# Activation tiles of a layer kernel moved by 8 to 256 bytes, and one product's columns walked backwards

## The chip, the core and the metric

The kernel runs on one core of one Trainium2 chip. The metric is the device time of one execution in microseconds (us); lower is better. Before the change the median of two runs is 2103.69 us (2103.62 to 2103.77).

## What is computed

One layer on a sequence of 256 rows of width 2048, in float32: a gated feed-forward block, a mixer with an attention branch and a gating branch, and a second feed-forward block. Cut to what matters here:

```python
x = x + 0.5 * swiglu(rms_norm(x, norm_ffn1), ffn1_w_gate, ffn1_w_up, ffn1_w_down)
h = rms_norm(x, norm_mix)
proj = h @ w_in                      # 2048 -> 10320 columns: q, k, v, index, u, v, gates
...                                  # attention with 64 picked keys; spatial gating
merged = sigmoid(ga) * (y_a @ w_up_attn) + sigmoid(gb) * (y_b @ w_up_sgu)
x = x + merged @ w_out
x = x + 0.5 * swiglu(rms_norm(x, norm_ffn2), ffn2_w_gate, ffn2_w_up, ffn2_w_down)
# swiglu(h, g, u, d) = (silu(h @ g) * (h @ u)) @ d ; inner width 5632
```

## The kernel before

Nearly all of the time goes into matrix products of 256 rows of activations with weights that are streamed from HBM once. One function, `gemm`, does each of them. For every block of 128 rows of the inner dimension (index `k`) the weights of 1024 output columns (1104 in one product) arrive by DMA in a tile `w`. ScalarE rounds them to the type float32r into `wh` (line 227), VectorE subtracts and writes what is left into `wl` (line 228). The activations are kept in the same manner as two float32r tiles, a high part and a low part, transposed: `xTh` and `xTl` hold the normed input of a stage (16 blocks of 128 by 256), `hTh` and `hTl` the inner activations of a feed-forward block (44 blocks).

A product of float32 accuracy is then three matrix products, lines 279 to 281: high activations by `wh`, low activations by `wh`, high activations by `wl`. In each, the activations are the stationary operand (128 by 128, loaded by a weight load of its own, LDWEIGHTS on PEld) and 512 columns of the weights are the moving operand (368 columns in the first product of the mixer). The result is added up in a PSUM bank `acc`. For one `k` there are two halves of the rows (`t`) and two blocks of columns (`j`), so 12 matrix products of 512 columns.

The stages stand one after the other:

- first block, gate and up: `acc<-wh,xTh` and its two companions, 11 chunks x 16 `k` x 12 = 2112 matrix products;
- first block, down: `acc<-wh,hTh`, 2 halves x 44 `k` x 12 = 1056;
- mixer, index columns: 288 of 368 columns, stationary operand from `xTh` and `xTl`;
- mixer, q, k, v, u, v and gates: 1728 of 512 columns from `xTh` and `xTl`, with the attention's small products strewn among them;
- mixer, three products with other activation tiles (`yah`, `ybh`, `mh`): 768;
- second block, gate and up: 2112; second block, down: 1056.

The class `Normed` makes `xTh` and `xTl` (lines 335 and 336 write them, ScalarE the high part and VectorE the low one). It is instantiated three times, for the first block, the mixer and the second block (`gi` is 0, 1 and 2), each time in the same memory. `ffn` makes `hTh` and `hTl`, written by lines 227 and 228 after a transposing DMA.

Where the tiles lie, in bytes from the start of a partition of SBUF, as the built program has it: `xTh` at 35840, `xTl` at 52224, the buffers of `wh` and `wl` from 93184 on in steps of 4096, `hTh` at 138240, `hTl` at 183296. All are multiples of 512. A stationary block is 512 bytes of a partition and begins at a multiple of 512; a moving block is 2048 bytes and begins 0 or 2048 bytes into a buffer (1472 bytes: 368 columns, at 0 or 1472). The distance between a moving and a stationary block, taken modulo 512 bytes, is 0 in every product of 512 columns.

Of the kernel before, what the change touches and what calls it, by code (L numbers as in the profile page):

```python
# [14 lines left out]
F32R = mybir.dt.float32r  # L15
# [6 lines left out]
P = 128  # L22
S = 256
NT = S // P
D = 2048
KD = D // P
FF = 5632
KF = FF // P
# [38 lines left out]
def block_kernel(ctx: ExitStack, tc: tile.TileContext, x, positions, norm_ffn1, ffn1_w_gate, ffn1_w_up,  # L67
# [5 lines left out]
    act = ctx.enter_context(tc.tile_pool(name="act", bufs=1))  # L73
# [9 lines left out]
    def uid(s):  # L83
        cnt[0] += 1
        return f"{s}_{cnt[0]}"

    def ttile(shape=None):
        return tmp.tile(shape or [P, 512], F32, tag="t", name=uid("t"))
# [4 lines left out]
    def bank(shape=None):  # L93
        return psA.tile(shape or [P, 512], F32, tag="acc", name=uid("acc"))
# [7 lines left out]
    def later(*stages):  # L102
        pending.extend(stages)

    def tick(n=1):
        for _ in range(min(n, len(pending))):
            pending.popleft()()
# [118 lines left out]
    def split_to(hi, lo, src):  # L226
        nc.scalar.copy(hi, src)  # L227
        nc.vector.tensor_sub(lo, src, hi.bitcast(F32))  # L228

    def gemm(xh, xl, nk, load, widths, first=0, rate=1, lead=None):  # L230

        ncol = sum(widths)
        kmax = 2048 // ncol
        banks = [[None] * len(widths) for _ in range(NT)]
        k0 = 0
        while k0 < nk:
            kg = min(1 if k0 < first else kmax, nk - k0)
            w = wraw.tile([P, 2048], F32, tag="w", name=uid("w"))
            wv = w[:, :kg * ncol].rearrange("p (k c) -> p k c", k=kg)
            load(k0, kg, wv)  # L240
            for kk in range(kg):
                k = k0 + kk

                offs = []
                o = 0
                for wd in widths:
                    offs.append(o)
                    o += wd
                parts = []
                cur = []  # L250
                for j, wd in enumerate(widths):
                    if cur and offs[j] + wd - offs[cur[0]] > 1024:
                        parts.append(cur)
                        cur = []
                    cur.append(j)
                parts.append(cur)
                hl = {}
                for part in parts:
                    a = offs[part[0]]
                    n = sum(widths[j] for j in part)  # L260
                    whi = wsp.tile([P, 1024], F32R, tag="wh", name=uid("wh"))
                    wlo = wsp.tile([P, 1024], F32R, tag="wl", name=uid("wl"))
                    with ExitStack() as order:
                        if lead is not None and k == 0:
                            for ins in lead:
                                order.enter_context(tc.issue_after(getattr(ins, "ins", ins)))
                        split_to(whi[:, :n], wlo[:, :n], wv[:, kk, a:a + n])
                    for j in part:
                        b = offs[j] - a
                        hl[j] = (whi[:, b:b + widths[j]], wlo[:, b:b + widths[j]])  # L270
                for t in range(NT):
                    sh = xh(k, t)
                    sl = xl(k, t)
                    for j, wd in enumerate(widths):
                        if k == 0:
                            banks[t][j] = bank()
                        o_ = banks[t][j][:, :wd]
                        whj, wlj = hl[j]
                        nc.tensor.matmul(o_, sh, whj, start=(k == 0), stop=False)  # L279
                        nc.tensor.matmul(o_, sl, whj, start=False, stop=False)  # L280
                        nc.tensor.matmul(o_, sh, wlj, start=False, stop=(k == nk - 1))  # L281
                tick(rate)
            k0 += kg
        return banks

    def loader(wap, c0, ncol):
        def load(k0, kg, dst):
            nc.sync.dma_start(dst, wap[k0 * P:(k0 + kg) * P, c0:c0 + ncol].rearrange("(k p) c -> p k c", p=P))
        return load
# [23 lines left out]
    class Normed:  # L313


        def __init__(self, gi):
            self.gi = gi
            self.h = act.tile([P, KD, S], F32R, tag="xTh", name=uid("xTh"))
            self.l = act.tile([P, KD, S], F32R, tag="xTl", name=uid("xTl"))
            self.ss = small.tile([P, NT, 4], F32, tag="ss", name=uid("ss"))  # L320
            self.rstd = small.tile([P, NT], F32, tag="rstd", name=uid("rstd"))

# [47 lines left out]
        def xh(self, k, t):  # L370
            return self.h[:, k, t * P:(t + 1) * P]

        def xl(self, k, t):
            return self.l[:, k, t * P:(t + 1) * P]

    def ffn(nrm, wg, wu, wd, after_chunk, first=0, lead=None):
        with tc.tile_pool(name=uid("ffn"), bufs=1) as pool:
            hTh = pool.tile([P, KF, S], F32R, name=uid("hTh"))
            hTl = pool.tile([P, KF, S], F32R, name=uid("hTl"))
            for fc in range(FF // 512):  # L380
                def load(k0, kg, dst, fc=fc):
                    for i, wap in enumerate((wg, wu)):
                        nc.sync.dma_start(dst[:, :, i * 512:(i + 1) * 512],
                                          wap[k0 * P:(k0 + kg) * P, fc * 512:(fc + 1) * 512].rearrange(
                                              "(k p) c -> p k c", p=P))
                b = gemm(nrm.xh, nrm.xl, KD, load, [512, 512], first=first if fc == 0 else 0, lead=lead if fc == 0 else None)
                for t in range(NT):
                    sg = ttile()
                    nc.scalar.activation(sg, b[t][0], AF.Silu, scale=nrm.rstd[:, t:t + 1])  # L389
                    hh = ttile()  # L390
                    nc.vector.scalar_tensor_tensor(hh, b[t][1], nrm.rstd[:, t:t + 1], sg,  # L391
                                                   op0=ALU.mult, op1=ALU.mult)
                    later(partial(turn_split, hTh[:, fc * 4:fc * 4 + 4, t * P:(t + 1) * P],
                                  hTl[:, fc * 4:fc * 4 + 4, t * P:(t + 1) * P], hh))
            for half in range(2):
                b = gemm(lambda k, t: hTh[:, k, t * P:(t + 1) * P], lambda k, t: hTl[:, k, t * P:(t + 1) * P],
                         KF, loader(wd, half * 1024, 1024), [512, 512])
                for t in range(NT):
                    for j in range(2):
                        xs = xres[:, t, (half * 2 + j) * 512:(half * 2 + j + 1) * 512]  # L400
                        nc.vector.scalar_tensor_tensor(xs, b[t][j], 0.5, xs, op0=ALU.mult, op1=ALU.add)  # L401
                        if t == NT - 1 or after_chunk is to_out:
                            after_chunk(half * 2 + j, t)
# [4 lines left out]
    lead = n1.pair(0)  # L408
# [19 lines left out]
    def to_out(c, t):  # L428
        nc.sync.dma_start(out[0, t * P:(t + 1) * P, c * 512:(c + 1) * 512], xres[:, t, c * 512:(c + 1) * 512])

    ffn(n1, ffn1_w_gate[0], ffn1_w_up[0], ffn1_w_down[0], to_mix, first=2, lead=lead)
    nm = nm[0]
    win = w_in[0]


    def mixer(pool, after_chunk):
# [30 lines left out]

        raw = mt("A", [P, NT, 1152], name="qik")
        b = gemm(nm.xh, nm.xl, KD, loader(win, C_QI, QIK), [368, 368, 368])
        flush()  # L470
        for t in range(NT):
# [297 lines left out]


    ffn(n2, ffn2_w_gate[0], ffn2_w_up[0], ffn2_w_down[0], to_out)


# [20 lines left out]
```

## Time and profile before

| | |
|---|---|
| median of two runs | 2103.69 us |
| the profiled execution | 2102.13 us |
| its span, first to last instruction | 2100.4 us |
| TensorE matmul (PE) busy | 2084.0 us, 99% |
| weight loads (PEld) busy | 1732.7 us, 82% |
| VectorE (DVE) busy | 1165.4 us, 55% |
| ScalarE (ACT) busy | 1038.5 us, 49% |
| HBM read | 398.26 MB |

How to read it: matrix products are pipelined, and the profile shows each from its start to the end of its last result, so that the time of one overlaps the next. A busy share of 99% says that there is always one under way, not how fast they follow each other. That is read from the distance between the starts of two neighbours in the timeline, or from the length of a stage over the number of its products.

### The profile page before, as it was taken

The page shows a single profiled execution, that of the slowest core. Times are in us where ns is not written, and L with a number is a line of the kernel's source. Part 1 is how long each engine was busy: PE and PEld are TensorE (multiplying, and loading weights), DVE is VectorE, ACT ScalarE, POOL GpSimd, SP SyncE. Part 2 cuts the span into 40 slices and gives each one's busy share as a digit, 9 for nine tenths or more (in the row PEclk, how much of TensorE's full clock was granted, in tenths as well). Part 3 has the DMA queues.
Part 4 walks back from the last instruction along what each step waited for, and adds up shares of the span by engine and source line. Part 5 has one row for each costly group of instructions (what it writes and reads, how often), then busy time and mean ns, then how long its engine had stood idle before and what let it go on. Part 6 is the DMA issues. An engine that isn't in the chain of part 4 may idle for free.

```text
span 2100.4 us, 24401 instructions
## 1 busy us (share of the span) xinstructions
PE 2084.0 (99%) x9318; PEld 1732.7 (82%) x9318; DVE 1165.4 (55%) x1362; ACT 1038.5 (49%) x1208; POOL 31.7 (2%) x60
## 2 busy tenths in 40 slices
PE   8999999999999999999999999999999999999998
PEld 6888888888888898888888888888888888888887
DVE  6555555555455457887544467555555555554443
ACT  5554444544345366567444445665444454443333
POOL 1000000000000000210000000000000000000000
PEclk9999999999999999999999999999999999999999
DMA  7666666666566477586665567676666666665654
GB/s 244 192 202 220 199 209 202 201 217 202 190 203 206 168 226 201 182 240 176 209 204 186 197 199 222 204 230 202 214 204 199 209 196 217 209 199 192 220 188 133
DMA packets 251526, 426.09 MB, mean 203 GB/s; under 512 B 106664, under 2 KB 108768, under 8 KB 251408
## 3 DMA queue, kind: packets, MB, share of 16 engines
q1 hardware_dynamic: 250880, 423.29, 63.7%
q0 software_dynamic: 528, 1.23, 0.3%
q8 instruction: 73, 1.20, 0.2%
q14 instruction: 45, 0.37, 0.1%
HBM read 398.26 MB, written 2.10 MB: 191 GB/s over the span
## 4 chain that ended last, share of the span: by engine, by line
PE 53%; ACT 0%; DMA 0%; DVE 0%; issue 0%; DVEq 0%
PE acc L279 17%; PE acc L281 17%; PE acc L280 17%; PE tr L687 0%; DMA tu<-pl 0%; DVE xres L401 0%; ACT L664 0%; PE tr L646 0%; ACT wh L227 0%; DVE pTs L299 0%; ACT vs L664 0%; DVEq L790 0%; ACT lgs L626 0%; ACT yah L227 0%; ACT pl L295 0%
## 5 line engine op out<-in xcount | busy, mean ns | idle before, releaser
L228 DVE TENSOR_TENSOR wl<-w,wh 128x1024 fp32r<-128x1024 f32 (+2 forms) x768 | 918.8, 1202 | 762.5 <-ACT wh L227 755.7
L227 ACT CAST wh<-w 128x1024 fp32r<-128x1024 f32 (+2 forms) x768 | 792.7, 1036 | 972.9 <-PE acc L280 957.3
L279 PE MATMUL acc<-wh,xTh 128*128 128x512 f32 (+1 forms) x2080 | 807.1, 388 | 3.4 <-ACT wh L227 3.4
L280 PE MATMUL acc<-wh,xTl 128*128 128x512 f32 (+1 forms) x2080 | 804.9, 387 | 0.0
L281 PE MATMUL acc<-wl,xTh 128*128 128x512 f32 (+1 forms) x2080 | 690.2, 387 | 0.0
L279 PEld LDWEIGHTS acc<-wh,xTh 128*128 128x128 f32 x2080 | 391.1, 188 | 81.8 <-ACT wh L227 4.7
L280 PEld LDWEIGHTS acc<-wh,xTl 128*128 128x128 f32 x2080 | 391.2, 188 | 76.6
L281 PEld LDWEIGHTS acc<-wl,xTh 128*128 128x128 f32 x2080 | 388.8, 188 | 77.3 <-DVE wl L228 0.6
L279 PE MATMUL acc<-wh,hTh 128*128 128x512 f32 x704 | 273.9, 389 | 0.0
L280 PE MATMUL acc<-wh,hTl 128*128 128x512 f32 x704 | 273.9, 389 | 0.0
L281 PE MATMUL acc<-wl,hTh 128*128 128x512 f32 x704 | 240.8, 389 | 0.0
L280 PEld LDWEIGHTS acc<-wh,hTl 128*128 128x128 f32 x704 | 132.2, 188 | 27.5
L281 PEld LDWEIGHTS acc<-wl,hTh 128*128 128x128 f32 x704 | 132.2, 188 | 27.4
L279 PEld LDWEIGHTS acc<-wh,hTh 128*128 128x128 f32 x704 | 132.2, 188 | 27.3
L299 DVE COPY t<-tu 128x1024 uint16<-128x1024 uint16 x60 | 45.6, 760 | 94.9 <-DMA tu<-pl 94.9
L295 ACT COPY pl<-t 128x1024 uint16<-128x1024 uint16 x58 | 60.4, 1043 | 0.4 <-DVE t L744 0.4
L280 PE MATMUL acc<-wh,ml 128*128 128x512 f32 x128 | 49.8, 389 | 0.0
L279 PE MATMUL acc<-wh,mh 128*128 128x512 f32 x128 | 49.6, 389 | 0.0
L281 PE MATMUL acc<-wl,mh 128*128 128x512 f32 x128 | 41.2, 389 | 0.0
L389 ACT ACTIVATE t<-acc,rstd 128x512 f32<-128x512 f32 x44 | 29.9, 690 | 10.7 <-PE acc L281 10.6
L391 DVE SCALAR_TENSOR_TENSOR t<-acc,rstd,t 128x512 f32<-128x512 f32 x44 | 32.0, 750 | 2.7 <-ACT t L389 2.7
L228 DVE TENSOR_TENSOR hTl<-t,hTh 128x512 fp32r<-128x512 f32 x44 | 30.2, 686 | 0.0
(182 smaller groups left out, 759.8 us busy)
## 6 DMA issues: line engine op xcount, KB each, us to landing
w<-in_ffn_w_down SPq DMA_DIRECT2D x88, 1024.0 KB, 5.1
w<-in_ffn_w_gate SPq DMA_DIRECT2D x175, 512.0 KB, 3.8
w<-in_ffn_w_up SPq DMA_DIRECT2D x175, 512.0 KB, 4.7
w<-in_w_in SPq DMA_DIRECT2D x72, 1024.0 KB, 5.0
w<-in_w_out SPq DMA_DIRECT2D x16, 1024.0 KB, 5.4
w<-in_w_in SPq DMA_DIRECT2D x16, 552.0 KB, 3.7
w<-in_w_up_attn SPq DMA_DIRECT2D x8, 1024.0 KB, 5.3
w<-in_w_up_sgu SPq DMA_DIRECT2D x8, 1024.0 KB, 5.4
```

What stands on the lines that cost most here:

```text
L227: nc.scalar.copy(hi, src)
L228: nc.vector.tensor_sub(lo, src, hi.bitcast(F32))
L279: nc.tensor.matmul(o_, sh, whj, start=(k == 0), stop=False)
L280: nc.tensor.matmul(o_, sl, whj, start=False, stop=False)
L281: nc.tensor.matmul(o_, sh, wlj, start=False, stop=(k == nk - 1))
L295: nc.scalar.copy(planes, src.bitcast(U16).rearrange("p (c h) -> p h c", h=2))
L299: nc.vector.tensor_copy(dst.bitcast(U16).rearrange("p j (c h) -> p h j c", h=2), turned)
L389: nc.scalar.activation(sg, b[t][0], AF.Silu, scale=nrm.rstd[:, t:t + 1])
L391: nc.vector.scalar_tensor_tensor(hh, b[t][1], nrm.rstd[:, t:t + 1], sg, op0=ALU.mult, op1=ALU.mult)
```

## The change

Three things change, all in where operands begin and in which direction they are read.

- `xTh` and `xTl` become two views into one tile `xT` of 2 x 4096 + 128 elements. They begin 4, 64 or 8 elements of 4 bytes into it: 16 bytes in the first block, 256 bytes in the mixer, 32 bytes in the second block. The buffers behind it move up by 512 bytes, so `wh`, `wl` and all tiles of the mixer still begin at multiples of 512.
- `hTh` and `hTl` become two views into one tile `hT`, which begin at its start in the first block and 2 elements (8 bytes) into it in the second.
- In the down product of the first block the moving operand and the result are walked from the last column to the first: column 511 of the weights goes in first, and its result into column 511 of the bank.

The distance modulo 512 bytes between stationary and moving blocks is thereby 16 (gate and up of the first block), 0 with the moving operand descending (down, first block), 256 (mixer, products from `xT`), 32 (gate and up, second block) and 8 (down, second block). The three mixer products with other activations keep 0.

The built programs have the same instructions in the same order on every engine, with the same operand shapes and the same waits, but for one: the third product of 368 columns in the mixer now also waits for a product that stands 531 places ahead of it on TensorE itself.

```diff
@@ gemm
-    def gemm(xh, xl, nk, load, widths, first=0, rate=1, lead=None):
+    def gemm(xh, xl, nk, load, widths, first=0, rate=1, lead=None, back=False):
...
                         whj, wlj = hl[j]
+                        if back:
+                            o_, whj, wlj = o_[:, ::-1], whj[:, ::-1], wlj[:, ::-1]
                         nc.tensor.matmul(o_, sh, whj, start=(k == 0), stop=False)
@@ Normed
-            self.h = act.tile([P, KD, S], F32R, tag="xTh", name=uid("xTh"))
-            self.l = act.tile([P, KD, S], F32R, tag="xTl", name=uid("xTl"))
+            both = act.tile([P, 2 * KD * S + 128], F32R, tag="xT", name=uid("xT"))
+            off = (4, 64, 8)[gi]
+            self.h, self.l = (both[:, off + i * KD * S:off + (i + 1) * KD * S].rearrange("p (k s) -> p k s", k=KD)
+                              for i in range(2))
@@ ffn
-            hTh = pool.tile([P, KF, S], F32R, name=uid("hTh"))
-            hTl = pool.tile([P, KF, S], F32R, name=uid("hTl"))
+            both = pool.tile([P, 2 * KF * S + 32], F32R, name=uid("hT"))
+            back = after_chunk is to_mix
+            off = 0 if back else 2
+            hTh, hTl = (both[:, off + i * KF * S:off + (i + 1) * KF * S].rearrange("p (k s) -> p k s", k=KF)
+                        for i in range(2))
...
-                         KF, loader(wd, half * 1024, 1024), [512, 512])
+                         KF, loader(wd, half * 1024, 1024), [512, 512], back=back)
```

## Rows read from the trace of the kernel before

**Rows 1.** The page: span, busy times of the engines.
```profile
span 2100.4 us, 24401 instructions
PE 2084.0 (99%) x9318; PEld 1732.7 (82%) x9318; DVE 1165.4 (55%) x1362; ACT 1038.5 (49%) x1208; POOL 31.7 (2%) x60
```

**Rows 2.** Stages: us, PE busy (products touched), PEclk, DMA share, GB/s.
```profile
10.64:495.25 484.61, 484.61 (x2139) 1.00 0.65 209
495.25:734.61 239.36, 239.36 (x1057) 1.00 0.58 194
734.61:786.28 51.67, 49.24 (x290) 1.00 0.78 225
786.28:1202.45 416.17, 415.95 (x1891) 1.00 0.64 200
1202.45:1376.53 174.08, 174.08 (x769) 1.00 0.69 212
1376.53:1855.25 478.72, 478.72 (x2113) 1.00 0.66 207
1855.25:2094.60 239.35, 239.35 (x1057) 1.00 0.58 187
```

**Rows 3.** Waits of PE: for whom, us in total, times, longest.
```profile
PE tr L328 <- DMA xres<-in_x: 4.2, 2, 3.4
PE acc L279 <- ACT wh L227: 3.4, 4, 1.1
```

**Rows 4.** Weight loads by line: busy us, mean ns of one, idle before.
```profile
L280 PEld LDWEIGHTS acc<-wh,xTl 128*128 128x128 f32 x2080 | 391.2, 188 | 76.6
```

**Rows 5.** Timeline of PE after four transposes: start us, us of each product.
```profile
29.90 0.48 PE L281 MATMUL acc<-wl,xTh 128*128 128x512 f32 x1
30.21 0.40 PE L280 MATMUL acc<-wh,xTl 128*128 128x512 f32 x1
30.45 0.40 PE L281 MATMUL acc<-wl,xTh 128*128 128x512 f32 x1
...
32.07 0.39 PE L279 MATMUL acc<-wh,xTh 128*128 128x512 f32 x1
32.29 0.39 PE L280 MATMUL acc<-wh,xTl 128*128 128x512 f32 x1
32.52 0.39 PE L281 MATMUL acc<-wl,xTh 128*128 128x512 f32 x1
...
33.88 0.39 PE L281 MATMUL acc<-wl,xTh 128*128 128x512 f32 x1
```

**Rows 6.** Timeline of PE, products of 368 columns in the mixer.
```profile
764.05 0.33 PE L279 MATMUL acc<-wh,xTh 128*128 128x368 f32 x1
...
766.90 0.33 PE L280 MATMUL acc<-wh,xTl 128*128 128x368 f32 x1
```

**Rows 7.** Timeline of PE near the start, products of 512 columns.
```profile
11.66 0.63 PE L279 MATMUL acc<-wh,xTh 128*128 128x512 f32 x1
12.09 0.63 PE L280 MATMUL acc<-wh,xTl 128*128 128x512 f32 x1
```

**Rows 8.** Lines that write the moved tiles: busy us, mean ns, idle before.
```profile
L228 DVE TENSOR_TENSOR hTl<-t,hTh 128x512 fp32r<-128x512 f32 x44 | 30.2, 686 | 0.0
L227 ACT CAST hTh<-t 128x512 fp32r<-128x512 f32 x44 | 27.1, 616 | 3.2 <-DVE t L299 3.0
L335 ACT ACTIVATE xTh<-t,gT 128x256 fp32r<-128x256 f32 x32 | 14.5, 502 | 0.0
L336 DVE SCALAR_TENSOR_TENSOR xTl<-t,gT,xTh 128x256 fp32r<-128x256 f32 x32 | 14.1, 481 | 3.2 <-ACT xTh L335 3.2
L336 DVE SCALAR_TENSOR_TENSOR xTl<-tr,gT,xTh 128x256 fp32r<-128x256 f32 x16 | 7.7, 480 | 5.9 <-ACT xTh L335 5.9
L335 ACT ACTIVATE xTh<-tr,gT 128x256 fp32r<-128x256 f32 x16 | 7.4, 467 | 5.4 <-PE tr L328 5.4
```

## The prediction

> **What bounds the kernel now.** I read the page first: PE is busy 99% of the span and no other engine over 55%, weight loads apart [rows 1]. Then the waits of PE, to see whether anybody holds it up: it waited 4.2 us for the input and 3.4 us for rounded weights, in the whole program [rows 3]. So no producer, no DMA and no order of work sets the time; what sets it is how fast matrix products follow one another. That number is in the table of stages: gate and up of the second block takes 478.72 us for 2112 products, 226.67 ns each; down takes 239.36 us in the first block and 239.35 us in the second for 1056 each, 226.67 ns; the three mixer products that the change leaves alone take 174.08 us for 768, again 226.67 ns [rows 2]. Gate and up of the first block is 5.9 us longer than its twin, which is its start-up. The reader is to see that four different stages, with other operands and other distances in time to ScalarE, VectorE and the DMAs (DMA share 0.58 to 0.69), have one and the same step to the hundredth of a nanosecond.
>
> What the step is made of: in the mixer's index product, 17 steps of 368 columns take 766.90 - 764.05 = 2.85 us, 167.65 ns each [rows 6]. [...] Each has a weight load of 188 ns in its shadow [rows 4]. [...] The rows after four transposes say no: from 30.21 to 32.29 us nine steps of the same kind of product take 2.08 us, 231.1 ns each (single ones 0.22 to 0.24), and then from 32.52 on six steps take 1.36 us, 226.7 ns each [rows 5]. [...]
>
> **The change part by part.** *Instructions.* None is added, removed or moved; the one added wait is for a product 531 places earlier, about 531 x 0.2267 = 120 us, long done: 0.
>
> *Writes to the moved tiles.* ScalarE and VectorE write `xT` and `hT` at the new offsets. All of it together is 27.1 + 14.5 + 7.4 = 49.0 us on ScalarE and 30.2 + 14.1 + 7.7 = 52.0 us on VectorE [rows 8], on engines with 1062 and 935 us free [rows 1]. I take 0: even at double length it would be hidden under PE, which has waited for none of these writes [rows 3]. Only the first pair at the start is uncovered (PE stood for it, ScalarE idle 5.4 us there); doubled, one write each of 467 and 480 ns, up to +1 us. If the cover were gone altogether, doubling would cost up to 101 us, but the waits give no sign of that.
>
> *The distance, in four stages.* 2112 products at 16 bytes, 1728 of 512 and 288 of 368 columns at 256 bytes, 2112 at 32 bytes, 1056 at 8 bytes. *The direction,* 1056 products. In sum 8064 steps of 512 columns that can move; the 768 others cannot. [...] I take that: +1.0 ns x 8064 = **+8.1 us**. The direction I put with the rest: backwards, the same addresses are read and the same bank columns written, each neighbour next to the last.
>
> [...]
>
> *Sum.* Own time of the profiled execution 2102.13 us (span 2100.4, and 1.7 us around it); +8.1 gives 2110.2 us. The median shown is 1.6 us above that execution, so I forecast 2111.8 us, rounded **2112 us**.
>
> **The rivals.**
>
> *Nothing moves.* The step stays 226.67 ns in all five stages: 2103.7 us. For it: the weight block is 512 bytes and the columns run past it in whole multiples of that, so any repeating pattern is gone through once whatever the start; and four stages have one step although the distance modulo 1024 alternates between 0 and 512 with `t`. [...]
>
> [...]
>
> *The streams don't settle.* If the five stages run as the nine unsettled steps do, +4.4 ns x 8064 = +35.7 us: 2139 us, still within 2%; at 0.24 us throughout, 2211 us. It is slower by 2% from +5.2 ns a step.
>
> *Backwards is dear.* The other side's single mechanism, at one place: down of the first block. If TensorE or PSUM handles a descending walk in smaller pieces, every column of 1056 products pays. The slowest steps of the trace with nothing between them are the first ones, 12.09 - 11.66 = 0.43 us [rows 7], 203 ns above the usual: 1056 x 203 ns = +215 us, 2318 us. It decides from 42.1 us / 1056 = 40 ns a product, a fifth of that. For it: nothing before is walked that way, so nothing excludes it. Against it: a step of one element remains a step of one element. [...]
>
> **How the numbers follow.** Chances: the small rise 0.38 (own range 2104 to 2140 us); nothing moves 0.22; a better step 0.14, of which 0.09 beyond 2%; no settling 0.13, of which 0.07 beyond 2%; backwards dear 0.13, nearly all beyond 2%. Two per cent, 42 us, is about what a measurement of this kernel can tell from no change. Faster: 0.09. Slower: 0.07 + 0.13 = 0.20. Within 2%: 0.71. The range leaves out the 0.09 below 2062 us (-2%), and above 2175 us most of the dear walk and the top of the unsettled case, about 0.10 more: 2062 to 2175 us.
>
> **What will show it.** The length of each stage over its products is the whole test. Right: PE still 99% busy with 7.6 us of waits, the untouched 768 products at 226.67 ns, gate and up near 227.7 ns (480.8 us in the second block), the two down products near 240.4 us. The dear walk would stand in the first down product alone, well above its twin's 239 us. Steps at 231 ns in one stage and 226.67 in another would say that the distance matters by its size; all at 226.67 that it doesn't matter. Wrong in kind I would be if PE's waits grew by more than a few us, since then the writes to the moved tiles had come onto the path. The prediction's size is wrong if a distance changes the settled value by several ns at once, which no row before can exclude.

## The result

The changed kernel takes 2128.26 us (median of two runs, 2128.10 to 2128.43) against 2103.69 us: a ratio of 1.0119, 95% interval 1.0094 to 1.0143. It is slower by 24.6 us, 1.2%, which stays within 2%. The forecast was 2112 us with a range of 2062 to 2175 us.

The page of the changed kernel, to be laid beside [rows 1]: the same number of instructions, busy times on VectorE and ScalarE within 1.2 us of those before, 26 us more of PE.

```profile
span 2126.3 us, 24401 instructions
PE 2109.7 (99%) x9318; PEld 1733.2 (82%) x9318; DVE 1166.6 (55%) x1362; ACT 1037.3 (49%) x1208; POOL 31.7 (1%) x60
```

PE's waits in the changed kernel (for whom, us in total, times, longest) have the totals of [rows 3] to the tenth of a microsecond. The 3.0 us for the identity at the start stand in the kernel before too, though [rows 3] leave them out; new are the 0.3 us in the attention:

```profile
PE tr L332 <- DMA xres<-in_x: 4.2, 2, 3.4
PE acc L281 <- ACT wh L227: 3.4, 4, 1.3
PE tr L140 <- POOL ident masks.py:199: 3.0, 1, 3.0
PE tr L625 <- DVE kT L301: 0.3, 1, 0.3
```

The stages of the changed kernel (us, PE busy with the products touched, PEclk, DMA share, GB/s) answer to [rows 2] line by line. From the top: gate and up of the first block (16 bytes), down of the first block (backwards), index product and the other products of the mixer from `xT` (256 bytes), the mixer's untouched 768, gate and up (32 bytes) and down (8 bytes) of the second block.

```profile
10.66:495.30 484.64, 484.64 (x2140) 1.00 0.65 209
495.30:741.70 246.40, 246.40 (x1057) 1.00 0.57 189
741.70:793.68 51.98, 49.53 (x290) 1.00 0.78 224
793.68:1210.14 416.46, 416.06 (x1891) 1.00 0.64 199
1210.14:1384.23 174.09, 174.09 (x769) 1.00 0.70 212
1384.23:1877.02 492.79, 492.79 (x2113) 1.00 0.66 201
1877.02:2120.60 243.58, 243.58 (x1057) 1.00 0.57 184
```

| stage | setting | before, us | after, us | difference | step, ns |
|---|---|---|---|---|---|
| gate and up, first | 16 bytes | 484.61 | 484.64 | +0.03 | 226.67 after the start-up |
| down, first | backwards | 239.36 | 246.40 | +7.04 | 233.33 |
| index product | 256 bytes | 51.67 | 51.98 | +0.31 | |
| mixer from `xT` | 256 bytes | 416.17 | 416.46 | +0.29 | 226.67 between disturbances |
| mixer, others | none | 174.08 | 174.09 | +0.01 | 226.67 |
| gate and up, second | 32 bytes | 478.72 | 492.79 | +14.07 | 233.33 |
| down, second | 8 bytes | 239.35 | 243.58 | +4.23 | 230.66 |

The differences sum to 25.98 us; the spans differ by 25.9. So the change's cost stands in three stages, and two settings of five, 16 and 256 bytes, cost next to nothing (0.03 and 0.60 us). The timeline of PE in the stage at 32 bytes (start us, us of each product) shows how a step of 233.33 ns looks: five steps, single ones of 0.23 or 0.24 us, take 1.17 us, and over the whole stage the mean is the same.

```profile
1500.66 0.40 PE L282 MATMUL acc<-wh,xT 128*128 128x512 f32 x1
...
1501.83 0.40 PE L281 MATMUL acc<-wh,xT 128*128 128x512 f32 x1
```

The change of step comes with the first products of the stage, without a wait: the first of these three lines is the last of the mixer's untouched products (`mh`, 226.67 ns apart on the average), the second is the first product of the second gate and up (`xT`), 0.23 us behind it. From there nine steps take 2.10 us, 233 ns each.

```profile
1384.00 0.40 PE L283 MATMUL acc<-wl,mh 128*128 128x512 f32 x1
1384.23 0.39 PE L281 MATMUL acc<-wh,xT 128*128 128x512 f32 x1
...
1386.33 0.40 PE L282 MATMUL acc<-wh,xT 128*128 128x512 f32 x1
```

Hereafter "step" is the length of a stage over its products (1056 in a down stage, 2112 in the second gate and up). The first gate and up and the mixer hold other products and the start-up as well. There the step is read from a stretch that nothing interrupts: of the first gate and up from about 100 to 480 us, 1627 to 1675 steps; of the mixer a run of 320 steps between two groups of the attention's small products. In the kernel before both stretches give 226.67 ns.

### The profile page after: what moved, and what is told of

The parts are those of the page before. It is cut to its first block, busy times and chain, and to the rows that moved or that the text cites. A ratio compares the mean times of both kernels' runs of the same rounds, so it can differ in the third digit from the quotient of the medians.

```text
span 2126.3 us, 24401 instructions
## 1 busy us (share of the span) xinstructions
PE 2109.7 (99%) x9318; PEld 1733.2 (82%) x9318; DVE 1166.6 (55%) x1362; ACT 1037.3 (49%) x1208; POOL 31.7 (1%) x60
## 4 chain that ended last, share of the span: by engine, by line
PE 96%; DMA 2%; DVE 1%; ACT 1%; issue 0%; POOL 0%; SPq 0%; DVEq 0%; ACTq 0%; POOLq 0%
PE acc L281 32%; PE acc L282 32%; PE acc L283 32%; DMA tu<-pl 1%; DMA xres<-in_x 0%; PE tr L625 0%; PE tr L653 0%; ACT wh L227 0%; DVE wl L228 0%; PE tr L694 0%; DVE k L585 0%; ACT pl L348 0%; PE tr L528 0%; PE tr L527 0%; PE tr L526 0%
## 5 line engine op out<-in xcount | busy, mean ns | idle before, releaser
L281 PE MATMUL acc<-wh,xT 128*128 128x512 f32 (+1 forms) x2080 | 812.1, 390 | 3.4 <-ACT wh L227 3.4
L282 PE MATMUL acc<-wh,xT 128*128 128x512 f32 (+1 forms) x2080 | 809.3, 389 | 0.0
L283 PE MATMUL acc<-wl,xT 128*128 128x512 f32 (+1 forms) x2080 | 694.9, 389 | 0.0
L281 PEld LDWEIGHTS acc<-wh,xT 128*128 128x128 f32 x2080 | 391.2, 188 | 86.9 <-ACT wh L227 4.9
L282 PEld LDWEIGHTS acc<-wh,xT 128*128 128x128 f32 x2080 | 391.3, 188 | 81.3
L283 PEld LDWEIGHTS acc<-wl,xT 128*128 128x128 f32 x2080 | 388.9, 188 | 81.8 <-DVE wl L228 0.6
L281 PE MATMUL acc<-wh,hT 128*128 128x512 f32 x704 | 278.2, 395 | 0.0
L282 PE MATMUL acc<-wh,hT 128*128 128x512 f32 x704 | 278.2, 395 | 0.0
L283 PE MATMUL acc<-wl,hT 128*128 128x512 f32 x704 | 244.9, 395 | 0.0
L283 PEld LDWEIGHTS acc<-wl,hT 128*128 128x128 f32 x704 | 132.3, 188 | 31.1
L281 PEld LDWEIGHTS acc<-wh,hT 128*128 128x128 f32 x704 | 132.3, 188 | 31.0
L282 PEld LDWEIGHTS acc<-wh,hT 128*128 128x128 f32 x704 | 132.3, 188 | 30.9
L228 DVE TENSOR_TENSOR hT<-t,hT 128x512 fp32r<-128x512 f32 x44 | 30.2, 686 | 0.0
```

## The experiments

Each takes the changed kernel and sets the offsets (in elements of 4 bytes) and directions anew. Since a stage's length is read from the profile by itself, one kernel tries five settings at once.

### The five settings change places

```diff
-            off = (4, 64, 8)[gi]
+            off = (8, 4, 64)[gi]
-            off = 0 if back else 2
+            off = 2 if one else 0
+            back = None if one else 'both'
```

> The five settings change places: 32 bytes in gate and up of the first block, 16 in the mixer, 256 in gate and up of the second, 8 in the first down, the backward walk in the second down. Theory, the distance alone sets the step: gate and up of the first block 498.7 us (484.6 + 2112 x 6.67 ns), of the second 478.7, first down 243.4, second down 246.4, mixer as before; in all about 2129 us. Rival, the cost belongs to the stage (its weights, its neighbours): second gate and up stays at 492.8 us and first down at 246.4 whatever their setting is.

2130.2 us. The stages: 32 bytes, 8 bytes, 16 bytes (mixer), 256 bytes, backwards:

```profile
10.38:508.41 498.03, 498.03 (x2140) 1.00 0.63 204
508.41:751.99 243.58, 243.58 (x1057) 1.00 0.57 191
803.93:1223.51 419.58, 419.15 (x1892) 1.00 0.63 198
1397.59:1876.32 478.73, 478.73 (x2114) 1.00 0.65 207
1876.32:2122.72 246.40, 246.40 (x1057) 1.00 0.56 182
```

Four costs moved along with the setting, to 0.7 us and less; the stage itself is not the cause. The mixer at 16 bytes was expected "as before" and took 3.4 us more. Its timeline shows why. Six small products of the attention stand between two runs of products from `xT`; before them the starts are 226.7 ns apart (nine steps from 845.67 to 847.71 take 2.04 us), after them 234 (ten from 848.88 to 851.22 take 2.34 us):

```profile
845.67 0.39 PE L282 MATMUL acc<-wh,xT 128*128 128x512 f32 x1
...
847.71 0.39 PE L282 MATMUL acc<-wh,xT 128*128 128x512 f32 x1
847.94 0.28 PE L527 MATMUL tr<-kih,qih 128*128 128x256 f32 x1
...
848.88 0.40 PE L281 MATMUL acc<-wh,xT 128*128 128x512 f32 x1
...
851.22 0.39 PE L282 MATMUL acc<-wh,xT 128*128 128x512 f32 x1
```

In the stretch of 320 steps later in the stage they are back at 226.67 ns. So at 16 bytes the same products have two steps that last, 226.7 and 234 ns, and here the step changed across the six small products.

### Everything 32 bytes higher, and the weights alone 32 bytes higher

```diff
-    const.tile([P, 24], F32, name="pad")
+    const.tile([P, 32], F32, name="pad")     # all tiles 32 bytes up, distances 0
```

> The kernel before with everything from the identity on 32 bytes higher: stationary and moving blocks both begin 32 bytes past a multiple of 512, distances all 0, nothing backwards. Theory, the distance decides: 226.67 ns a step in all stages, 2103.7 us. [...]

2104.02 us, beside 2103.39 for the kernel before. The first down and the mixer's other products:

```profile
496.51:735.87 239.36, 239.36 (x1057) 1.00 0.58 194
1204.07:1378.15 174.08, 174.08 (x769) 1.00 0.69 212
```

```diff
-    small.tile([P, 32], F32, tag="pad", bufs=1, name="pad")
+    wsp.tile([P, 8], F32, tag="pad", bufs=1, name="wpad")    # wh, wl 32 bytes up
+    small.tile([P, 24], F32, tag="pad", bufs=1, name="pad")  # and what follows back in place
```

> Activations at multiples of 512 bytes, the buffers of the rounded weights 32 bytes higher: the distance is minus 32 bytes in every stage, the three mixer products with other activations among them. Theory, the distance modulo 64 bytes or less decides: 233.33 ns in all 8832 products of 512 columns, +58.9 us, 2162.6 us. Rival, the place of the stationary block decides: 226.67 ns, 2103.7 us. If the sign of the distance matters: neither value.

2161.05 us. The first down, the mixer's other products, the second gate and up:

```profile
509.94:756.34 246.40, 246.40 (x1057) 1.00 0.57 189
1235.19:1414.39 179.20, 179.20 (x770) 1.00 0.67 206
1414.39:1907.19 492.80, 492.80 (x2114) 1.00 0.63 201
```

All of them at 233.33 ns, the 768 products too, whose activations no variant moves. In the first of the two kernels both blocks lie 32 bytes higher and nothing is lost; in the second the moving ones alone do, and every stage pays. That settles what the quantity is: where the two operands lie to each other, not how either is aligned. The first kernel has the merged tiles `xT` and `hT` as well, so the merging is not the cause.

### Which part of walking backwards costs

Distances 0; in the down products the rounded weights are stored in reverse, so that reading and writing can be turned apart.

```diff
-                        split_to(whi[:, :n], wlo[:, :n], wv[:, kk, a:a + n])
+                        src = wv[:, kk, a:a + n]
+                        split_to(whi[:, :n], wlo[:, :n], src[:, ::-1] if back in ("read", "write") else src)
...
+                        if back in ("both", "write"):
+                            o_ = o_[:, ::-1]
+                        if back in ("both", "read"):
+                            whj, wlj = whj[:, ::-1], wlj[:, ::-1]
```

> All distances 0. In both down stages the rounded weights are stored in reverse; the first down reads them from the last to the first and writes the bank forwards, the second reads them forwards and writes the bank from the last column to the first. Theory, the direction of the reading stream against that of the weight load costs the 6.67 ns: first down 246.4 us, second 239.35 us, in all 2110.7 us. Rival, the descending write into PSUM costs it: first 239.4, second 246.4 us. If either alone is free and only the pair costs: 239.4 in both, 2103.7 us.

2108.42 us. First down (read backwards), second down (written backwards):

```profile
494.87:741.27 246.40, 246.40 (x1057) 1.00 0.56 189
1861.53:2100.88 239.35, 239.35 (x1057) 1.00 0.57 187
```

The descending read costs all of the 7.04 us, the descending write into PSUM nothing.

### A map of distances, and backwards at other distances

```diff
-            off = (4, 64, 8)[gi]
+            off = (1, 6, 10)[gi]       # then (16, 32, 3), (4, 12, 8), (11, 24, 15)
-            off = 0 if back else 2
+            off = 12 if one else 14    # then 5, 7; 2, 12; 9, 13
```

In the third of the four kernels gate and up are given `back` as well, so that all four feed-forward products are walked backwards.

> Nothing backwards; distances 4 bytes (first gate and up), 24 (mixer), 40 (second gate and up), 48 (first down), 56 (second down). Theory, the step depends on the distance modulo 64 bytes and alike on both sides of 0: 48 bytes as 16 (226.67 ns, 239.4 us), 56 as 8 (230.5 ns, 243.4 us), 24 and 40 alike (for 40: 478.7 to 492.8 us, between the 226.67 of 16 and the 233.33 of 32). Rival, the period is 32 bytes or less: impossible for 32 itself, but 48 as 16 and 56, 40, 24 all as 8 bytes, 230.5 ns. Rival, no period this short: 48 and 56 bytes above 233.33 ns. 4 bytes: 226.67 to 230.5 ns.

> Nothing backwards; distances 64 bytes (first gate and up), 128 (mixer), 12 (second gate and up), 20 (first down), 28 (second down). Theory, modulo 64 bytes: 64 and 128 bytes as 0, 484.6 us and the mixer as before; 12 and 20 bytes around 16, between 226.67 and 230.5 ns; 28 bytes near 32, 230.5 to 233.33 ns (243.4 to 246.4 us). Rival, a longer period (256 bytes, at which nothing was lost): 64 or 128 bytes cost, up to 233.33 ns, 498.7 us in the first stage.

> All four feed-forward products walked backwards, at distances 16 bytes (first gate and up), 32 (second), 8 (first down), 48 (second down); mixer forwards at 48. Theory, backwards only shifts what the distance means (a descending walk begins 2044 bytes up, 60 modulo 64): some of the four fall back to 226.67 ns (gate and up 478.7 us, down 239.4). Rival, the direction itself costs 6.67 ns at any distance, since the streams then run against each other: 233.33 ns or more in all four (492.8 and 246.4 us). The mixer at 48 as at 16 or 0: 416 to 420 us.

> Nothing backwards; distances not tried yet: 44 bytes (first gate and up), 96 (mixer), 60 (second gate and up), 36 (first down), 52 (second down). Theory, 226.67 ns is the least step of any distance: each stage between 226.67 and 233.33 ns, the whole 2104 to 2155 us. Rival, some distance settles lower, at 220 ns: gate and up 464.6 us in the second block, down 232.3 us, which would make a faster kernel.

| run, us | gate and up, first | mixer | gate and up, second | down, first | down, second |
|---|---|---|---|---|---|
| first map, 2134.12 | 4 bytes: 232.4 ns | 24: 231.1, later 230.1 | 40: 226.67 | 48: 233.33 | 56: 233.33 |
| second map, 2132.50 | 64: 233.33 | 128: 232.4 | 12: 226.67 | 20: 233.33 | 28: 226.67 |
| backwards, 2155.16 | 16 back: 233.33 | 48 forwards: 233.33 | 32 back: 233.33 | 8 back: 233.33 | 48 back: 233.33 |
| third map, 2149.15 | 44: 230.0 | 96: 234.3 | 60: 233.33 | 36: 233.33 | 52: 233.33 |

The stretches at 44, 24, 128 and 96 bytes (x counts one or two products more than there are steps, those that the ends of the stretch cut):

```profile
100.01:479.97 379.96, 379.96 (x1654) 1.00 0.65 203
879.04:952.99 73.95, 73.95 (x321) 1.00 0.70 207
881.69:956.05 74.36, 74.36 (x321) 1.00 0.70 206
874.71:949.68 74.97, 74.97 (x322) 1.00 0.70 204
```

The period of 64 bytes is refuted: 64 bytes cost 6.7 ns, and 48 is not as 16. So are the shorter periods. Nothing in the map is smooth, 12, 28 and 40 bytes are free between neighbours that cost, and no setting goes below 226.67 ns. The other bound of the last expectation, 233.33 ns, did not hold: 96 bytes lie above it. Backwards, all four settings are at 233.33 ns, as in the three stages read backwards above: seven of seven, at five distances. There the rival held: the direction costs 6.67 ns a product at each distance tried.

### The low activations further off than the high ones

```diff
-            off = (4, 64, 8)[gi]
+            off, low = (0, 0, 0)[gi], (8, 0, 4)[gi]     # low part that much further
-            off = 0 if back else 2
+            off, low = 0, 2 if one else 16
```

> Nothing backwards; the high activations at distance 0, the low ones further off: by 32 bytes in the first gate and up, 16 in the second, 8 in the first down, 64 in the second down; so one weight load in three stands at another distance. Theory, each load costs by its own distance: first gate and up 484.6 + 2112 x 6.67/3 = 489.3 us, first down 240.7, the others as before. Rival, a changing distance keeps the streams from settling: around 231 ns a step, first gate and up 493.8 us, first down 243.9, second gate and up 487.9. Rival, the loads of the high part alone matter: all as before.

2122.34 us. First gate and up (every third load 32 bytes off) 496.53 us, 232.5 ns a step; first down (8 bytes) 243.82 us, 230.9 ns; second gate and up (16 bytes) 478.72 us, 226.67 ns; second down (64 bytes) 242.90 us, 230.0 ns. A third of the loads at 32 bytes brings not a third of the cost but nearly nine tenths of it. The costs of single loads do not add up; the theory of a load that costs by its own distance is out. Of its rivals neither holds in all stages.

### Distances that cost nothing, in other stages

```diff
-            off = (4, 64, 8)[gi]
+            off = (10, 64, 3)[gi]      # then (7, 10, 4)
-            off = 0 if back else 2
+            off = 3 if one else 10     # then 4 in both
```

> Distances other than 0 alone, of those that cost nothing so far, most of them in a stage where they have not been: 40 bytes (first gate and up), 256 (mixer), 12 (second gate and up), 12 (first down), 40 (second down); nothing backwards. Theory, the distance alone decides which step the streams settle at: 226.67 ns in all stages, 484.6, 239.4, 416.2, 478.7 and 239.35 us, 2103.7 us, the same as before. Rival, the stage or what came before it decides: some stages at 230 to 233.33 ns, up to +50 us.

2124.33 us, ratio 1.0101 (95% interval 1.0084 to 1.0118), and not by the theory. Its five runs took 2143.20, 2124.46, 2124.14, 2124.33 and 2124.33 us: one program, 19 us between two of its executions, where seven runs of the kernel before beside it lie between 2102.38 and 2104.16 us. The profile is of the longest. Its stages at 40, 12, 256, 12 and 40 bytes, in order of time:

```profile
10.50:508.75 498.25, 498.25 (x2139) 1.00 0.64 203
508.75:755.15 246.40, 246.40 (x1057) 1.00 0.57 189
807.20:1223.17 415.97, 415.88 (x1891) 1.00 0.64 200
1397.25:1889.34 492.09, 492.09 (x2114) 1.00 0.65 201
1889.34:2135.74 246.40, 246.40 (x1057) 1.00 0.56 182
```

The very setting that was free in the second map (12 bytes, second gate and up: 226.67 ns) is here at 233.0 ns on the average. Its timeline shows the moment. The stage begins with products 226.67 ns apart; from 1421.51 us on, with no idle time of PE that the profile shows, the starts slip, and from there to the end they are 233.3 ns apart:

```profile
1421.28 0.39 PE L282 MATMUL acc<-wh,xT 128*128 128x512 f32 x1
1421.51 0.39 PE L283 MATMUL acc<-wl,xT 128*128 128x512 f32 x1
1421.74 0.40 PE L281 MATMUL acc<-wh,xT 128*128 128x512 f32 x1
1421.97 0.40 PE L282 MATMUL acc<-wh,xT 128*128 128x512 f32 x1
1422.21 0.39 PE L281 MATMUL acc<-wh,xT 128*128 128x512 f32 x1
```

What stands at that moment in the rows of the weight loads is a late load. Elsewhere in this stage a load starts with the product that runs over it, as at 1421.28. That of 1421.58 alone starts 0.07 us behind the product of 1421.51, and ScalarE had ended the rounding of a `wh` 0.05 us before (1420.49 + 1.04):

```profile
1420.49 1.04 ACT L227 CAST wh<-w 128x1024 fp32r<-128x1024 f32 x1
1421.28 0.19 PEld L283 LDWEIGHTS acc<-wl,xT 128*128 128x128 f32 x1
1421.58 0.19 PEld L281 LDWEIGHTS acc<-wh,xT 128*128 128x128 f32 x1
```

In the second map the same stage at 12 bytes has no late load and stays at 226.67 ns throughout. At distance 0 a longer disturbance does not last: in the kernel with everything 32 bytes higher a load of the second gate and up waits 0.37 us for its rounded weights, and the stage returns to 226.67 ns and takes 478.96 us.

```profile
1402.74 0.19 PEld L281 LDWEIGHTS acc<-wh,xT 128*128 128x128 f32 x1 [0.37 <-ACT wh L227]
```

Each was seen once, so that the late load set off the slip is likely and not shown. Without the slip the stage would be 13.4 us shorter; of the faster executions there is no trace, so where they saved their 19 us is not shown.

> 16 bytes in three stages that have not had it (second gate and up, both down products), 28 bytes in the first gate and up, 40 in the mixer. With 16 bytes the streams settled at 226.67 ns in one stage and, after each of the mixer's small products, now at 226.67 and now at 233.33. Theory, the distance has two lasting states and what came before picks one: each of the three stages is wholly at 226.67 (478.7, 239.4 us) or wholly at 233.33 ns (492.8, 246.4 us), and not all of them need be alike. Rival, one state, and the mixer's small products alone disturb it: 226.67 in all three. Mixer at 40: 416 us.

2122.44 us. The three stages at 16 bytes are wholly at 226.67 ns (second gate and up 478.72 us, downs 239.36 and 239.35); the first gate and up at 28 bytes is at 233.33 ns (498.31 us), where 28 bytes had been free in a down stage. The mixer at 40 bytes takes 423.08 us instead of 416 and has both steps in one stage, 226.7 ns over 320 steps and later 233.5 over 695:

```profile
872.76:945.30 72.54, 72.54 (x322) 1.00 0.69 204
1060.15:1222.40 162.25, 162.25 (x698) 1.00 0.57 191
```

So the three stages came out as the rival said, which the theory allowed as well; that a distance by itself does not name one step is shown by the mixer.

### Shorter weight loads

```diff
+                        if 0 < k < nk - 1:
+                            o_, sh, sl = o_[:m], sh[:, :m], sl[:, :m]
                         nc.tensor.matmul(o_, sh, whj, start=(k == 0), stop=False)
...
-                         KF, loader(wd, half * 1024, 1024), [512, 512], back=back)
+                         KF, loader(wd, half * 1024, 1024), [512, 512], m=64 if one else 32)
```

> Distances 0. The down products load a part of the activations only, for all inner blocks but the first and the last: 64 of 128 columns in the first block, 32 in the second; the other rows of the result are left without most of their sum. The moving operand has its 512 columns as before. [...]

2112.15 us, beside 2103.47 for the kernel before: longer, not shorter. The loads themselves did shrink, from the 188 ns of [rows 4] (line, engine, op, shape, count, busy us, mean ns):

```profile
L284 PEld LDWEIGHTS acc<-wh,hT 128*64 128x64 f32 x336 | 45.1, 134 | 31.9
L285 PEld LDWEIGHTS acc<-wl,hT 128*32 128x32 f32 x336 | 36.6, 109 | 41.2
```

The first down took 242.79 us, 229.9 ns a step, the second 244.51 us, 231.5 ns. So a load of half the columns, or of a quarter, does not bring a shorter step, and the step is not the same for every load either. The full load at distance 0 keeps the shortest step that any run showed, 226.67 ns. The edit also narrows the result to 64 or 32 rows; which of the two made the step longer is not shown.

## Why the prediction was right, and where not

*The bound.* Right: PE is busy 99% and waits for others as long as before; all of the difference is in the step of the matrix products, stage by stage. The 7.6 us of waits that the prediction counted are 10.6 with the 3.0 us for the identity, in both kernels.

*Instructions and writes.* Right at 0. The writes to the moved tiles take 27.2 + 14.5 + 7.4 us on ScalarE and 30.2 + 14.1 + 7.7 us on VectorE in the changed kernel, as in [rows 8] within 0.1 us.

*The distance, +1.0 ns for each of 8064 products.* The sign was right and the size was a third of the true one: +25.9 us instead of +8.1 (7.04 of it for the direction), and not spread, but 0, 6.67, 0, 6.66 and 4.0 ns a product in five stages. No run shows the +1.0 ns, which was the author's estimate from the index product; what the runs showed in its place are these five values, lasting steps of 226.67, 230.66 and 233.33 ns. The step that failed is the choice of the nearest row. In the index product two blocks of columns in three still stand at distance 0, and the third, 1472 bytes into the buffer, at 64; its 167.65 ns is a mean over both [rows 6]. Wherever 64 bytes were tried they cost more: 233.33 ns a step as the constant distance of a stage, 230.0 ns where one load in three had it. In [rows 5] the step goes from 231.1 to 226.7 ns after nine steps, and a stage with one constant distance can stay at one value for a thousand products and more, as the second gate and up did at 233.33 ns over 2112. The price of a long stage was to be had only as one of a few lasting values. Of the prediction's own figures the mean of the unsettled rows, +4.4 ns, lay nearest to the 4.0 and 6.67 ns measured. It did name this way of being wrong: a distance that changes the settled value by several ns at once.

*The direction, put with the rest.* Failed: +6.67 ns for each of 1056 products, 7.04 us, of which the read is all and the write nothing. The argument that the same addresses are read had nothing to do with the cause. The rival that it would be dear needed 40 ns a product, 6 times what it cost. What made the 0.43 us of [rows 7], from which that rival took its price, is not shown; the profile gives a granted clock of 1.00 over those first products. Where it gives 0.50, in the index product of the kernel with everything 32 bytes higher, after PE had waited 1.45 and 0.21 us for rounded weights, seven steps of 368 columns take 2.14 us, 306 ns each, against the 167.65 ns of [rows 6] at 1.00:

```profile
753.70:756.90 3.20, 3.20 (x12) 0.50 0.81 210
754.04 0.51 PE L281 MATMUL acc<-wh,xT 128*128 128x368 f32 x1
...
756.18 0.51 PE L282 MATMUL acc<-wh,xT 128*128 128x368 f32 x1
```

*What is shown of the cause.* Moving the weights alone by 32 bytes put the first down, the mixer's other products and the second gate and up at 233.33 ns and cost 57.7 us in all; moving both operands by 32 bytes cost 0.6 us. The descending read cost 6.67 ns a product. What makes TensorE lose the time inside is not shown by any run; that it hangs on where the two operands lie to each other, and on the direction of the read, is shown by which moves cost and which do not.

*Nothing moves.* Its argument, that a repeating pattern is gone through once whatever the start, is refuted by 32 bytes at 233.33 ns in three kernels. *A better step:* in none of some 40 stages that ran forwards at a constant distance other than 0 was the mean step below 226.67 ns by more than 0.1 ns. No kernel here beats the one before. *No settling:* the step does settle, on values of the size that this rival took from the unsettled rows (231.1 ns); three of five stages went there.

*The range.* It held because its upper end left room for the unsettled case, which was priced for all stages at once. The likeliest case's own range, 2104 to 2140 us, held too, but that was luck: no row told that 16 and 256 bytes would cost nothing. With all 8064 products at 233.33 ns, as many other distances gave, the time would have been about 2157 us.

## What to carry to other kernels

Where matrix products with a weight load each follow one another without waits, read the step as stage length over product count and compare it between stages: in a stage that is 3% off at equal shapes, look first at the distance of its two operands in SBUF and at the direction in which the moving one is read. Keep the moving and the stationary blocks at the same place modulo 512 bytes and ascending: distance 0 kept the shortest step, 226.67 ns, in every stage that had it with full weight loads and was read forwards, and of the other settings only 256 bytes did so too, in the three stages tried. Do not price a lasting state by a row that shows an unsettled one, and do not take one stage's good luck with another distance for a property of that distance.

## What the runs showed of the hardware

- The step of a 512-column float32r product with its own weight load took lasting means of 226.67, 230.0 to 232.4, 233.33 and, at 96 bytes, 234.3 ns, according to the distance between its operands, at a granted clock of 1.00 throughout. 32 bytes gave 233.33 ns in the second gate and up of the changed kernel (492.79 us for 2112 products) and in the three stages shown with the weights alone 32 bytes higher; 0 bytes, read forwards and with full weight loads, gave 226.67 ns.
- At 12, 16, 28 and 40 bytes two lasting steps were seen, 226.67 ns and 233.3 to 234. At 12 bytes, from a weight load on that started 0.07 us late, 226.67 ns became 233.3 for the rest of the stage; at distance 0 the step came back to 226.67 ns after a load that waited 0.37 us. One program with such distances varied by 19 us between executions.
- A descending read of the moving operand gave 233.33 ns in seven stages of seven; with a descending write into PSUM a down stage took 239.35 us, as before.
- Weight loads of 64 and 32 columns took 134 and 109 ns instead of 188, and the step became longer, 229.9 and 231.5 ns. What the step consists of stays open. At a granted clock of 0.50 a product of 368 columns took 306 ns a step, at 1.00 it took 167.65.
